# A hybrid decoder trunk on one core: VectorE and ScalarE of the last matrix product put in program order, its loads begun earlier, and the residual added in PSUM

## The chip, the cores and the metric

The kernel runs on one core of a Trainium2 chip. The metric is the device time of one execution in microseconds (us). A time worked on by the profiler ("the profiled execution") is given with its span, which reaches from the first to the last instruction.

The core has five engines with an instruction queue each: TensorE (PE in the rows, with its weight loads as PEld) multiplies into PSUM, VectorE (DVE) and ScalarE (ACT) do elementwise work, GpSimd (POOL) little here, and SyncE (SP) issues all DMA transfers.

## What is computed

One decoder layer in float32 on 1024 positions of width 1024: a token mixer, cross-attention, a gated MLP with a causal convolution, and a final RMSNorm. The change lies in the last two lines of this excerpt.

```python
def conv_ffn(xn, w_up, conv_w, conv_b, w_down):
    h = xn @ w_up                                   # 1024 x 5632
    hp = jnp.pad(h, ((0, 0), (CONV_WIDTH - 1, 0), (0, 0)))
    hc = conv_b + sum(conv_w[k] * hp[:, k:k + S] for k in range(CONV_WIDTH))
    gate, val = jnp.split(hc, 2, axis=-1)
    return (jax.nn.silu(gate) * val) @ w_down       # 2816 -> 1024
...
    h = h + conv_ffn(xn, ...)
return rmsnorm(h, final_norm_g)
```

## The kernel before

**Split operands.** A float32 product is done in three TensorE products: each operand is split into a high part (`hi`, a ScalarE copy that rounds, L150) and a low part (`lo = src - hi`, a VectorE subtraction, L151), and `mm3` (L138) adds hi·hi, hi·lo and lo·hi in PSUM. So before TensorE can take an operand, ScalarE and then VectorE have to pass over it. The first of three matmuls needs only `hi`, the second `lo`.

**The up phase** makes the MLP's inner activations in 11 chunks `c` of 256 features, for `kind` 0 (gate) and 1 (value). Each is seven products of one weight block by one block of activations (`pair`, L734; the names B11, B21, T2, T3, T1, T4, B22 are operand blocks that lie in `slot` buffers). After the seven products the convolution follows (`conv`: a ScalarE shift L700, two VectorE taps L701 and L702, then for kind 1 the gate product L707 and the store of the chunk to DRAM, L708).

**The down phase** multiplies these activations by `w_down`. It is a seven-product scheme of 2x2 blocks too: the products p1, p7, p6, p4, p5, p2 and p3 each run over the 11 chunks. Counted on, that is 77 steps, and this text numbers them 0 to 76 (p1 is 0 to 10, p7 11 to 21, p6 22 to 32, p4 33 to 43, p5 44 to 54, p2 55 to 65, p3 66 to 76). A step is 12 matmuls (`multiply`, four PSUM banks of three). The four banks `bank` and the four banks `val` take turns, product by product.

Per chunk there is a large buffer `G[c]` (four pieces of 128x512) and a small one `U[c]` (two pieces), which reuse the buffers of the up phase's operands. They are filled by `load_first` (two pieces), `load_second` (three) and `load_third` (one), 256 KB a piece, 66 pieces in all. VectorE then forms the sums that a product needs in place, by line L903 (`sub`), L913 and L924; three of these functions (`p6`, `p5`) also issue the reload of a piece.

**Order.** TensorE and SP run in program order throughout. VectorE and ScalarE are ordered by a scheduler, which places instructions by their dependencies and by `tc.high_priority()`. `run` (L936) asks for the operands of the next two steps, sums included, at high priority:

```python
        for c in range(NC - whole):
            ahead(2)
            w = ops.pop(c)
            for i in range(4):
                multiply(banks[i], w, i, fresh and c == 0, c == NC - 1, not fresh)
```

The operands go into four sets in turn (two pairs of `wb`, two pairs of `tb`). SP's order at the start is: the first loads of chunks 0 to 3, then the two stores of the last activations, then the rest.

**End.** After each product, `add_res` (L387) adds the four banks to the residual `res` in SBUF. At the end the last three steps are done bank by bank; for each bank follow `add_res`, a square with row sum (ScalarE L985), a small VectorE operation (L986), a power on GpSimd (L987), two scalings (ScalarE L988 and VectorE L989) and two stores (L992).

Of the kernel before, what the change touches and what calls it, by code (L numbers as in the profile page):

```python
# [15 lines left out]
P = 128  # L16
D = 1024
# [12 lines left out]
def kernel(ctx: ExitStack, tc: tile.TileContext, a, out: bass.AP):  # L30
# [842 lines left out]
    nset = [0]  # L873

    def operands(*srcs):

        i = nset[0] % 4
        nset[0] += 1
        if i < 2:
            hi, lo = wb[2 * i], wb[2 * i + 1]  # L880
        else:
            renew_temp(2 * i - 4, F32R)
            renew_temp(2 * i - 3, F32R)
            hi, lo = tb[2 * i - 4], tb[2 * i - 3]
        with tc.high_priority():
            if len(srcs) == 1:
                v = lambda x: x.rearrange("p (q n) -> p q n", q=2)
                split(srcs[0], v(hi), v(lo))
            else:
                for q in range(2):  # L890
                    split(srcs[q], hi[:, q * 512 : (q + 1) * 512], lo[:, q * 512 : (q + 1) * 512])
        return hi, lo
# [6 lines left out]
    def evict(t, n, banks, i):  # L899
        with tc.high_priority():  # L900
            add_res(4 * t + i, n, banks[i])

    sub = lambda o, x, y: nc.vector.tensor_tensor(o, x, y, ALU.subtract)  # L903

    def p1(c):
        return (G[c][:, 0:2],)

    def p7(c):
        sub(U[c], U[c], G[c][:, 0::3])
        return (U[c],)  # L910

    def p6(c):
# [3 lines left out]
        return (U[c],)  # L916

    def p4(c):
        sub(G[c][:, 1], G[c][:, 1], U[c][:, 1])
        return G[c][:, 2], G[c][:, 1]  # L920

    def p5(c):
# [4 lines left out]
        return (G[c][:, 0:2],)  # L927

    def p2(c):
        return G[c][:, 2], U[c][:, 1]  # L930

    def p3(c):
        sub(G[c][:, 2], G[c][:, 2], U[c][:, 0])
        return (G[c][:, 2:4],)

    def run(prep, banks, fresh, outs, steps=(), whole=0):  # L936

        ops = {}
        todo = list(range(NC))

        def ahead(n):
            while todo and len(ops) < n:
                c = todo.pop(0)
                with tc.high_priority():
                    ops[c] = operands(*prep(c))

        for c in range(NC - whole):
            ahead(2)
            w = ops.pop(c)
            for i in range(4):  # L950
                multiply(banks[i], w, i, fresh and c == 0, c == NC - 1, not fresh)
            for f in steps:
                f(c)
        ahead(whole)
        for i in range(4):
            for c in range(NC - whole, NC):
                multiply(banks[i], ops[c], i, False, c == NC - 1, not fresh)
            for t, n in outs:
                evict(t, n, banks, i)
            if whole:  # L960
                last(i)
# [3 lines left out]
    early = {}  # L965

    def free(c):
        return slot[big_tags[c]][:, :1024]

    def first_half(i):  # L970

        c = slice(0, 512)
        o, ss = free(4 + i), tiny()
        early[i] = free(8 + i // 2)[:, i % 2 * 512 : i % 2 * 512 + 512]
        nc.scalar.activation(o[:, c], res[i][:, c], AF.Square, accum_out=ss)
        sums[i] = tiny()
        nc.vector.tensor_scalar(sums[i], ss, D * EPS, None, ALU.add)
        tt(early[i], res[i][:, c], gF[:, c], ALU.mult)

    def last(i):  # L980
        o, r = free(4 + i), res[i]
        v, ss, rs = tiny(), tiny(), tiny()
        with tc.high_priority():
            c = slice(512, D)
            nc.scalar.activation(o[:, c], r[:, c], AF.Square, accum_out=ss)  # L985
            nc.vector.tensor_scalar(v, ss, sums[i], 1.0 / D, ALU.add, ALU.mult)  # L986
            nc.gpsimd.tensor_tensor(rs, v, mhalf, ALU.pow)  # L987
            nc.scalar.activation(o[:, :512], early[i], AF.Copy, scale=rs)  # L988
            nc.vector.scalar_tensor_tensor(o[:, c], r[:, c], rs, gF[:, c], ALU.mult, ALU.mult)  # L989
        for q in range(2):  # L990
            c = slice(q * 512, (q + 1) * 512)
            nc.sync.dma_start(out[i * P : (i + 1) * P, c], o[:, c])  # L992

    def whole_tile(i):
        o, r = free(i - 4), res[i]
        v, ss, rs = tiny(), tiny(), tiny()
        nc.scalar.activation(o, r, AF.Square, accum_out=ss)
        nc.vector.tensor_scalar(v, ss, 1.0 / D, EPS, ALU.mult, ALU.add)
        nc.gpsimd.tensor_tensor(rs, v, mhalf, ALU.pow)
        nc.vector.scalar_tensor_tensor(o, r, rs, gF, ALU.mult, ALU.mult)  # L1000
        nc.sync.dma_start(out[i * P : (i + 1) * P], o)

    def second_ahead(c):
        if c + 5 < NC:
            load_first(c + 5)
        load_second(c)

    def early_loads(q):
        if 1 <= q <= 4:
            load_first(q - 1)  # L1010

    for c in range(1, NC):
        pair(0, c)
        pair(1, c, early_loads if c == NC - 1 else None)
    load_first(4)
    run(p1, bank, True, [(0, 0)], [second_ahead])
    run(p7, val, True, [(1, 1)], [load_third])
# [66 lines left out]
```

## Time and profile before

| | |
|---|---|
| median of 3 runs | 1202.66 us (1202.23 to 1204.57) |
| profiled execution: its time | 1205.13 us |
| its span | 1203.4 us |
| TensorE busy | 1168.1 us (97%) |
| VectorE busy | 789.4 us (66%) |
| ScalarE busy | 512.1 us (43%) |
| DMA | 105.37 MB, 88 GB/s on average |
| mean granted TensorE clock | 0.988 of full |
| chain that ended last | TensorE 90%, DMA 4%, VectorE 4% |

Busy TensorE is not TensorE at its peak: the matmuls are pipelined and overlap, so the rows below are read by when matmuls start and by the idle time ahead of them. The down phase is the last fifth of the span; everything ahead of it has TensorE busy at 9 tenths or more of each slice.

### The profile page before, as it was taken

The numbers are of one execution on the slowest core, as the hardware profiler recorded it, in microseconds if no ns is written. First come the engines' busy times: TensorE is split into PE (matmuls) and PEld (weight loads), VectorE is DVE, ScalarE is ACT, GpSimd is POOL, SyncE is SP. The second block draws the span as 40 slices with busy tenths as digits, with TensorE's granted clock in tenths as the row PEclk, the third lists the DMA queues.
The fourth block names the chain that finished last, engine by engine and source line by source line (L and its number), as shares of the span: only waits on it lengthen the run. The fifth ranks groups of instructions, "written<-read, shape, count | busy, mean of one in ns | idle before, by whom it ended". The sixth has DMA issues, their size and how long they took to land.

```text
span 1203.4 us, 14229 instructions
## 1 busy us (share of the span) xinstructions
PE 1168.1 (97%) x5512; PEld 978.4 (81%) x5512; DVE 789.4 (66%) x1074; ACT 512.1 (43%) x811; POOL 34.2 (3%) x75
## 2 busy tenths in 40 slices
PE   9999999999999999999999999999999976799997
PEld 7888888899888888888888888888888865688885
DVE  5555852258534524459878878787887769866684
ACT  7422322246423412356545545455454532244543
POOL 1200100100000000000000000000000000000000
PEclk9999999999999999999999999999999988899999
DMA  9211131155100111101222132212322295124011
GB/s 350 91 44 52 53 106 68 39 174 175 37 1 1 55 68 36 36 1 35 88 88 79 62 105 88 88 61 79 105 88 88 88 357 202 62 76 135 1 70 70
DMA packets 43844, 105.37 MB, mean 88 GB/s; under 512 B 4992, under 2 KB 5120, under 8 KB 43776
## 3 DMA queue, kind: packets, MB, share of 16 engines
q1 hardware_dynamic: 43776, 104.46, 25.0%
q8 instruction: 43, 0.70, 0.2%
q14 instruction: 25, 0.20, 0.0%
HBM read 88.72 MB, written 15.73 MB: 87 GB/s over the span
## 4 chain that ended last, share of the span: by engine, by line
PE 90%; DMA 4%; DVE 4%; issue 1%; ACT 1%; SPq 0%; POOL 0%; POOLq 0%; ACTq 0%; DVEq 0%
PE sm L136 46%; PE bank L136 24%; PE big L136 18%; PE sm L144 2%; DMA slot<-in_w_down_dram 1%; DMA h<-act 1%; DMA slot<-act 1%; DVE wb L151 1%; DMA h<-in_w_down_dram 1%; DVE tb L151 0%; DVE h L913 0%; SPq L157 0%; DVE slot L924 0%; DMA h<-in_w_v_dram 0%; DVE slot L903 0%
## 5 line engine op out<-in xcount | busy, mean ns | idle before, releaser
L136 PE MATMUL sm<-slot,wb 128*128 128x512 f32 (+1 forms) x1176 | 219.6, 346 | 0.0
L150 ACT CAST wb<-raw 128x512 fp32r<-128x512 f32 (+1 forms) x178 | 113.5, 641 | 238.8 <-PE sm L136 59.5
L136 PEld LDWEIGHTS sm<-slot,wb 128*128 128x128 f32 x1176 | 188.6, 189 | 27.2
L136 PE MATMUL big<-slot,wb 128*128 128x512 f32 (+1 forms) x704 | 180.0, 377 | 0.0
L151 DVE TENSOR_TENSOR wb<-raw,wb 128x512 fp32r<-128x512 f32 (+1 forms) x178 | 126.3, 712 | 66.5 <-ACT wb L150 66.2
L136 PE MATMUL bank<-slot,wb 128*128 128x512 f32 x696 | 161.6, 389 | 0.0
L136 PEld LDWEIGHTS bank<-slot,wb 128*128 128x128 f32 x696 | 130.5, 188 | 27.0
L136 PEld LDWEIGHTS big<-slot,wb 128*128 128x128 f32 x704 | 125.5, 188 | 23.9 <-DVE tb L336 0.7
L136 PE MATMUL sm<-slot,slot 128*128 128x512 f32 x376 | 91.8, 395 | 1.2 <-ACT slot L150 1.2
L387 DVE TENSOR_TENSOR res<-res,sm 128x512 f32<-128x512 f32 x44 | 29.6, 687 | 95.9 <-PE sm L136 95.9
L136 PEld LDWEIGHTS sm<-slot,slot 128*128 128x128 f32 x376 | 71.5, 191 | 16.8 <-ACT slot L150 1.5
L136 PE MATMUL sm<-h,slot 128*128 128x512 f32 x264 | 66.0, 391 | 0.0
L701 DVE SCALAR_TENSOR_TENSOR slot<-tb,par,slot 128x1023 f32<-128x1023 f32 x44 | 56.3, 1282 | 10.7 <-ACT slot L700 9.7
L136 PE MATMUL big<-h,wb 128*128 128x512 f32 x160 | 62.3, 389 | 0.0
L136 PE MATMUL bank<-wb,wb 128*128 128x512 f32 x176 | 57.5, 409 | 2.8 <-DVE wb L151 2.8
L136 PEld LDWEIGHTS sm<-h,slot 128*128 128x128 f32 x264 | 49.3, 188 | 10.1
L136 PE MATMUL sm<-wb,wb 128*128 128x512 f32 x136 | 43.1, 398 | 14.7 <-DVE wb L151 14.7
L136 PE MATMUL bank<-tb,tb 128*128 128x512 f32 x176 | 54.6, 391 | 2.4 <-DVE tb L151 2.4
L702 DVE SCALAR_TENSOR_TENSOR slot<-tb,par,slot 128x1022 f32<-128x1022 f32 x44 | 56.2, 1278 | 0.0
L700 ACT ACTIVATE slot<-tb,par 128x1024 f32<-128x1024 f32 x44 | 54.7, 1244 | 3.3 <-DVE tb L737 2.6
L136 PE MATMUL bank<-h,wb 128*128 128x512 f32 x240 | 56.0, 389 | 0.0
L136 PE MATMUL sm<-h,wb 128*128 128x512 f32 x240 | 56.0, 389 | 0.0
(180 smaller groups left out, 1721.8 us busy)
## 6 DMA issues: line engine op xcount, KB each, us to landing
raw<-in_w_up_dram SPq DMA_DIRECT2D x88, 256.0 KB, 3.3
act<-h SPq DMA_DIRECT2D x22, 512.0 KB, 3.0
slot<-act SPq DMA_DIRECT2D x33, 256.0 KB, 5.4
slot<-in_w_down_dram SPq DMA_DIRECT2D x33, 256.0 KB, 5.4
h<-in_w_down_dram SPq DMA_DIRECT2D x20, 256.0 KB, 4.9
res<-in_x_dram SPq DMA_DIRECT2D x8, 512.0 KB, 10.2
raw<-in_w_pu_dram SPq DMA_DIRECT2D x8, 512.0 KB, 3.9
raw<-in_w_out_dram SPq DMA_DIRECT2D x8, 512.0 KB, 3.5
```

The costliest lines, as they stand in the source:

```text
L136: i = nc.tensor.matmul(o, l, r, start=start, stop=stop, skip_group_check=more)
L144: i = nc.tensor.transpose(o, i_, ident)
L150: copied[0] = nc.scalar.copy(hi, src)
L151: nc.vector.tensor_tensor(lo, src, f32(hi), ALU.subtract)
L387: nc.vector.tensor_tensor(r, r, ps, ALU.add)
L700: nc.scalar.activation(o, h, AF.Identity, bias=w(3), scale=w(2))
L701: stt(o[:, 1:], h[:, : S - 1], w(1), o[:, 1:], ALU.mult, ALU.add)
L702: stt(o[:, 2:], h[:, : S - 2], w(0), o[:, 2:], ALU.mult, ALU.add)
```

## The change

For the down phase and the last chunk of the up phase, VectorE and ScalarE are taken from the scheduler and run in program order as well. That order is then written out: in step `t`, the split of step `t + 3`, the sums for step `t + 5`, the matmuls of step `t`, and whatever a table `later` lists for `t` (evictions, loads, the parts of the final norm). The operand sets are given by a list `sets`, of which the first steps use three and then four. The last value chunk is written out too, with the down phase's first loads and splits between its products. Ahead of the last product, `seed` adds the residual to the accumulating PSUM banks; the last square and the last scaling read PSUM, and there is no last `add_res`.

```diff
+    sets = [(tb, 0), (wb, 0), (wb, 2)] * 2 + [(tb, 2)]
+    sets += [(tb, 0), (wb, 0), (wb, 2), (tb, 2)] * 18
...
-    def p7(c):
+    def sum7(c):
         sub(U[c], U[c], G[c][:, 0::3])
...
+    STEPS = 7 * NC
+    AHEAD, SUMS = 3, 5
...
+    def step(t):
+        k, c = divmod(t, NC)
+        banks, fresh = products[k][2:4]
+        w = ops.pop(t)
         for i in range(4):
+            multiply(banks[i], w, i, fresh and c == 0, c == NC - 1, not fresh)
+        for f, args in later[t]:
+            f(*args)
...
+    def seed(i):
+        tt(bank[i], bank[i], res[i][:, 512:], ALU.add)
...
+    def last_square(i):
+        v, ss, rs = tail[i] = tiny(), tiny(), tiny()
+        nc.scalar.activation(free(4 + i)[:, 512:], bank[i], AF.Square, accum_out=ss)
+        nc.vector.tensor_scalar(v, ss, sums[i], 1.0 / D, ALU.add, ALU.mult)
         nc.gpsimd.tensor_tensor(rs, v, mhalf, ALU.pow)
+    def last_scale(i):
+        nc.scalar.activation(o[:, :512], early[i], AF.Copy, scale=rs)
+        nc.vector.scalar_tensor_tensor(o[:, c], bank[i], rs, gF[:, c], ALU.mult, ALU.mult)
...
+    at(2, load_first, 10)
+    at(2, load_second, 10)
+    for c in range(3, 10):
+        at(c - 3, load_second, c)
+    for c in range(NC):
+        at(c + 8, load_third, c)
...
+    ctx.enter_context(tc.manual_schedule(engines={ET.DVE, ET.Activation}))
...
+    go(0, X, "B11")
+    load_first(0)
+    load_first(1)
+    nc.scalar.copy(c11, X)
...
+    for t in range(STEPS - 3):
+        reuse = sets[t + AHEAD] == sets[t]
+        if t == 1:
+            taps0()
+        if reuse:
+            step(t)
+        prepare_step(t + AHEAD)
+        if t == 1:
+            gate0()
+        sum_step(t + SUMS)
+        if not reuse:
+            step(t)
+    for i in range(4):
+        for t in range(STEPS - 3, STEPS):
+            multiply(bank[i], ops[t], i, False, t == STEPS - 1, True)
+        last_square(i)
+        if i:
+            last_scale(i - 1)
+    last_scale(3)
```

On SP, where the down phase's loads begin. Before: the first loads of chunk 3 (`slot_6558`), the two stores of the last activations, and then the first loads of chunks 4 and 5 and the second loads of chunk 0 (`h_0_6621`).

```order
L157 DMA slot_6558<-act_0_3737 128x512
L157 DMA slot_6558<-in_w_down_dram 128x512
L708 DMA act_1_3752<-h_1_4118 128x1024
L708 DMA act_0_3751<-h_0_4117 128x1024
L157 DMA slot_6599<-act_0_3739 128x512
L157 DMA slot_6599<-in_w_down_dram 128x512
L157 DMA slot_6618<-act_0_3741 128x512
L157 DMA slot_6618<-in_w_down_dram 128x512
L157 DMA h_0_6621<-act_0_3731 128x512
```

Now, the same engine around the same two stores: the first loads of chunk 9 (`slot_6626`) and the second loads of chunks 3 and 4 (`h_1_6647`, `slot_6517`, `h_0_6667`, `slot_6535`) stand ahead of the second store, and behind it the first loads of chunk 10 (`slot_6687`).

```order
L157 DMA slot_6626<-act_0_3749 128x512
L157 DMA slot_6626<-in_w_down_dram 128x512
L1065 DMA act_1_3752<-h_1_4118 128x1024
L157 DMA h_1_6647<-act_0_3737 128x512
L157 DMA h_1_6647<-in_w_down_dram 128x512
L157 DMA slot_6517<-in_w_down_dram 128x512
L157 DMA h_0_6667<-act_0_3739 128x512
L157 DMA h_0_6667<-in_w_down_dram 128x512
L157 DMA slot_6535<-in_w_down_dram 128x512
L1065 DMA act_0_3751<-h_0_4117 128x1024
L157 DMA slot_6687<-act_0_3751 128x512
L157 DMA slot_6687<-in_w_down_dram 128x512
```

The first loads of chunks 4 to 9 and the second loads of chunks 0 to 2 moved from behind both stores to ahead of them.

On VectorE, in the second half of p7 (steps 11 to 21). Before: the stretch that ends with the splits of step 18 (`tb_6939<-h_1_6770`, chunk 7) and step 17 (`wb_76<-h_0_6752`, chunk 6). L913 is a sum of p6, L924 one of p5 (steps 44 to 54), L903 the subtraction of any of these products; the split of step 20 (chunk 9, `h_1_6808`) stands three rows ahead of this piece.

```order
L913 TENSOR_TENSOR h_1_6808<-slot_6706,h_1_6808 128x512
L903 TENSOR_TENSOR slot_6558<-slot_6558,h_1_6688 128x512
L903 TENSOR_TENSOR h_1_6732<-slot_6618,h_1_6732 128x512
L903 TENSOR_TENSOR h_1_6808<-slot_6706,h_1_6808 128x512
L924 TENSOR_TENSOR slot_6506<-slot_6506,h_0_6621 128x512
L924 TENSOR_TENSOR slot_6706<-slot_6706,h_1_6808 128x512
L924 TENSOR_TENSOR slot_6599<-slot_6599,h_0_6709 128x512
L151 TENSOR_TENSOR tb_6939<-h_1_6770,tb_6938 128x1024
L924 TENSOR_TENSOR slot_6542<-slot_6542,h_0_6667 128x512
L913 TENSOR_TENSOR h_1_6770<-slot_6664,h_1_6770 128x512
L924 TENSOR_TENSOR slot_6685<-slot_6685,h_0_6788 128x512
L151 TENSOR_TENSOR wb_76<-h_0_6752,wb_75 128x1024
```

Now, on the same engine, the splits of steps 17 to 20: by the new buffers `h_0_6716` is chunk 6, `h_1_6734` chunk 7, `h_0_6752` chunk 8 and `h_1_6771` chunk 9. L899 is the subtraction of any sum, here p7's, and L387 an eviction of p1.

```order
L151 TENSOR_TENSOR wb_76<-h_0_6716,wb_75 128x1024
L899 TENSOR_TENSOR h_0_6752<-h_0_6752,slot_6623 128x1024
L387 TENSOR_TENSOR res_66<-res_66,bank_3730 128x512
L151 TENSOR_TENSOR tb_6701<-h_1_6734,tb_6700 128x1024
L899 TENSOR_TENSOR h_1_6771<-h_1_6771,slot_6626 128x1024
L151 TENSOR_TENSOR tb_6570<-h_0_6752,tb_6569 128x1024
L899 TENSOR_TENSOR misc<-misc,slot_6687 128x1024
L151 TENSOR_TENSOR wb_74<-h_1_6771,wb_73 128x1024
```

The splits now stand in the order of the steps, with one step's sums between two of them.

## Rows read from the trace of the kernel before

**Rows 1.** Busy time by stretch: PE, PEld, DVE, ACT, POOL, clock, DMA share, GB/s.
```profile
954.70:1194.60 239.90, 217.47 (x925) 177.04 (x924) 177.07 (x227) 90.95 (x121) 3.44 (x6) 0.95 0.33 118
954.70:1048.00 93.30, 70.87 (x280) 55.98 (x280) 78.41 (x93) 26.97 (x26) 0.00 (x0) 0.87 0.57 206
1048.00:1194.60 146.60, 146.59 (x647) 121.06 (x645) 98.67 (x135) 63.98 (x95) 3.44 (x6) 1.00 0.18 62
```

**Rows 2.** Timeline of PE, first to last matmul of the down phase: start, duration, [idle before].
```profile
954.75 0.39 PE L136 MATMUL bank<-wb 128*128 128x512 f32 x1
...
964.05 0.73 PE L136 MATMUL bank<-tb,tb 128*128 128x512 f32 x2 [0.75 <-DVE tb L151]
...
969.33 0.80 PE L136 MATMUL bank<-wb 128*128 128x512 f32 x1 [2.49 <-ACT wb L150]
970.59 1.22 PE L136 MATMUL bank<-wb,wb 128*128 128x512 f32 x2 [0.46 <-DVE wb L151]
...
973.32 1.06 PE L136 MATMUL bank<-wb,wb 128*128 128x512 f32 x2
...
989.40 0.90 PE L136 MATMUL bank<-wb,wb 128*128 128x512 f32 x2 [2.33 <-DVE wb L151]
...
1027.78 1.22 PE L136 MATMUL sm<-wb,wb 128*128 128x512 f32 x2 [14.74 <-DVE wb L151]
...
1047.62 0.73 PE L136 MATMUL bank<-tb,tb 128*128 128x512 f32 x2 [1.64 <-DVE tb L151]
...
1193.98 0.61 PE L136 MATMUL bank<-wb,wb 128*128 128x512 f32 x2
```

**Rows 3.** Timeline of ACT: the splits of step 27 and of step 76.
```profile
1050.52 1.05 ACT L150 CAST tb<-h 128x1024 fp32r<-128x1024 f32 x1 [3.68 <-PE bank L136]
...
1183.75 1.05 ACT L150 CAST wb<-slot 128x1024 fp32r<-128x1024 f32 x1 [1.67 <-PE bank L136]
```

**Rows 4.** Timelines of ACT and DVE around step 17.
```profile
1004.74 1.05 ACT L150 CAST wb<-h 128x1024 fp32r<-128x1024 f32 x1 [1.71 <-PE sm L136]
1008.65 3.70 DVE L913 TENSOR_TENSOR h<-slot,h 128x512 f32<-128x512 f32 x6
1026.49 1.24 DVE L151 TENSOR_TENSOR wb<-h,wb 128x1024 fp32r<-128x1024 f32 x1
```

**Rows 5.** Waits of SP's queue (total us, times, longest), then timeline of ACT.
```profile
SPq L708 <- DVE h L707: 19.0, 2, 17.0
968.24 1.04 ACT L150 CAST wb<-slot 128x1024 fp32r<-128x1024 f32 x1 [5.50 <-DMA slot<-in_w_down_dram]
```

**Rows 6.** Timeline of DVE in the last up chunk, around its convolution's start.
```profile
952.23 0.69 DVE L737 TENSOR_TENSOR tb<-tb,sm 128x512 f32<-128x512 f32 x1 [0.34 <-PE sm L136]
...
954.46 1.28 DVE L701 SCALAR_TENSOR_TENSOR slot<-tb,par,slot 128x1023 f32<-128x1023 f32 x1 [1.54 <-ACT slot L700]
```

**Rows 7.** DMA issues (KB each, us to landing), then timeline of SP's queue.
```profile
act<-h SPq DMA_DIRECT2D x22, 512.0 KB, 3.0
slot<-act SPq DMA_DIRECT2D x33, 256.0 KB, 5.4
995.35 7.10 SPq L157 DMA_DIRECT2D slot<-act  x11
```

**Rows 8.** Timeline of DVE: two splits one right behind the other.
```profile
1045.21 1.23 DVE L151 TENSOR_TENSOR wb<-h,wb 128x1024 fp32r<-128x1024 f32 x1
1046.34 1.23 DVE L151 TENSOR_TENSOR tb<-h,tb 128x1024 fp32r<-128x1024 f32 x1
```

**Rows 9.** Timeline of DVE and ACT at the end: the last bank.
```profile
1196.13 0.75 DVE L989 SCALAR_TENSOR_TENSOR slot<-res,small,raw 128x512 f32<-128x512 f32 x1 [0.66 <-POOL small L987]
1196.80 0.68 DVE L387 TENSOR_TENSOR res<-res,bank 128x512 f32<-128x512 f32 x1
1197.51 0.63 ACT L985 ACTIVATE slot<-res 128x512 f32<-128x512 f32 x1 [0.66 <-DVE res L387]
1199.14 0.75 DVE L989 SCALAR_TENSOR_TENSOR slot<-res,small,raw 128x512 f32<-128x512 f32 x1 [0.66 <-POOL small L987]
```

More of the change, by code (lines that the diff above doesn't have):

```diff
@@ L977, in first_half @@
         nc.vector.tensor_scalar(sums[i], ss, D * EPS, None, ALU.add)
[L978 to L998, printed above, removed]
-        nc.gpsimd.tensor_tensor(rs, v, mhalf, ALU.pow)
[L1000 to L1006, printed above, removed]
@@ new lines @@
+    at(2, load_first, 10)
[4 more added lines that the diff above has]
+        at(c + 8, load_third, c)
+    at(20, load, gF, a["gF"].broadcast_to([P, D]))
+    for k in range(6):
+        for i in range(4):
+            for t, n in products[k][4]:
+                at((k + 1) * NC + i, add_res, 4 * t + i, n, products[k][2][i])
+    for i in range(4):
+        at(57 + 2 * i, square, 4 + i)
+        at(58 + 2 * i, power, 4 + i)
+        at(59 + 2 * i, scaled, 4 + i)
+        at(59 + i, seed, i)
+        at(67 + i, first_half, i)
@@ L1027, with go, add, conv_parts @@
-    run(p3, bank, False, [(0, 1)], whole=3)
+        if c < NC - 1:
+            pair(1, c)
+    ctx.enter_context(tc.manual_schedule(engines={ET.DVE, ET.Activation}))
+    c10 = NC - 1
+    X, Z, Y, V = val
+    (c11, c12), (c21, c22) = (hl(H[1][j]) for j in range(2))
+    def go(q, o, xname, start=True):
+        product(o, ready.pop((1, c10, q)), xname, start, True, not start)
+        prepare()
+    def add(o, x):
+        tt(o, o, x, ALU.add)
+    def conv_parts(j):
+        h, f = H[1][j], NF + 2 * c10 + j
+        w = lambda q: pconv[:, f, q : q + 1]
+        o = half(0, j)
+        stt = nc.vector.scalar_tensor_tensor
+        sg = half(7, j)
+        def shift():
+            nc.scalar.activation(o, h, AF.Identity, bias=w(3), scale=w(2))
+        def taps():
+            stt(o[:, 1:], h[:, : S - 1], w(1), o[:, 1:], ALU.mult, ALU.add)
+            stt(o[:, 2:], h[:, : S - 2], w(0), o[:, 2:], ALU.mult, ALU.add)
+        def gate():
+            tt(sg, sg, o, ALU.mult)
+            nc.sync.dma_start(act[c10][j], sg)
+        return shift, taps, gate
@@ new lines @@
+    shift0, taps0, gate0 = conv_parts(0)
+    shift1, taps1, gate1 = conv_parts(1)
+    go(0, X, "B11")
+    load_first(0)
+    load_first(1)
+    nc.scalar.copy(c11, X)
+    go(1, Z, "B21")
+    load_first(2)
+    load_first(3)
+    add(c11, Z)
+    go(2, X, "T2", False)
+    load_first(4)
+    load_first(5)
+    nc.scalar.copy(c21, X)
+    go(3, Y, "T3")
+    for c in range(3):
+        load_second(c)
+    add(c21, Y)
+    prepare_step(0)
+    go(4, X, "T1", False)
+    nc.scalar.copy(c22, X)
```

145 lines of the change are left out of this document (75 added, 70 removed).

## The prediction

> **What bounds the kernel now.** I read the busy time by stretch first. From the first matmul of the down phase to its last, 239.9 us pass, and they fall into two parts [rows 1]: up to 1048 us TensorE is busy for 70.87 of 93.3 us at a mean granted clock of 0.87; behind it for 146.59 of 146.6 us at 1.00. So whatever a change of order can give back lies in the first 93 us. VectorE is busy for 177.1 us of the whole stretch, less than TensorE needs, so it isn't the bound by its sum; by its order it may be.
>
> The pace without stalls comes from ScalarE. In the second part its split of each step is released by TensorE's end of a step, so the distance of two splits is the length of a step: from step 27 to step 76 there are 49 steps in 1183.75 - 1050.52 = 133.23 us, 2.72 us each [rows 3]. The phase has 77 steps: 77 x 2.72 = 209.44 us, plus 0.16 us by which the last matmul (0.39 us) outlasts the distance to a next one (2.72/12 = 0.23). It took from 954.75 to 1193.98 + 0.61 = 1194.59, 239.84 us [rows 2]. The excess is 239.84 - 209.60 = 30.24 us.
>
> Then TensorE's timeline, for where the excess lies. There are six idle pieces, and the rows of the group are all of them: 0.75 + 2.49 + 0.46 + 2.33 + 14.74 + 1.64 = 22.41 us [rows 2]. [...] Each idle microsecond so cost 7.83/22.41 = 0.35 us more, and I price idle time at 1.35.
>
> What ended the long gap is the `lo` of step 17. ScalarE had its `hi` done at 1004.74 + 1.05 = 1005.8; VectorE made the `lo` at 1026.49, and in between it did work for later products, such as six sums of p6 (step 22 on) in one row [rows 4]. It was never waiting in that time; the order held the split back. The three gaps at 964 to 971 have another origin: SP waited 17.0 us at the first store of the last activations, with the first loads of chunks 4 to 10 behind it in its queue, and ScalarE then waited 5.50 us for step 4's data [rows 5].
>
> **The change, part by part.**
>
> *Order of VectorE and ScalarE.* It removes no work but the last four `add_res`; each split and sum remains. Costs for VectorE, from two splits in a row: 1.23 us each, 1.13 from start to start [rows 8]; 128x512 sums start 0.60 apart (six in 3.70, each 0.70) [rows 4]. Per step this makes 1.13 + 1.13 = 2.26 us in p7's range, 1.13 + 1.20 = 2.33 where p6's sums are made, and 0.60 more in the four steps that carry an eviction, 2.93 at most. Over 2.72 by 0.21, four times, VectorE falls behind by 0.8 us and makes it up at 0.39 a step. The densest place is steps 59 to 63 (p2's split 1.20, a seed 0.60, a scaling 1.2 every other step, from step 61 a sum 0.60): about 14.05 us against 5 x 2.72 = 13.6, 0.45 behind. How much lateness can it bear? With four operand sets, ScalarE's split of step t+3 starts as step t starts on TensorE, `hi` takes 1.05 [rows 3] and `lo` 1.23, so it is ready 2.28 us into step t; the second matmul of t+3 wants it at 3 x 2.72 + 0.23 = 8.39. Slack 6.1 us, against 0.8 needed. So the 14.74, 2.33 and 1.64 us gaps go, and nothing is late next: sums stand five steps ahead, two before their split.
>
> *The start.* With three sets the slack is smaller, so I follow VectorE with full durations. The add of the T4 product starts at 952.23 and the taps at 954.46, as before [rows 6]: taps to 954.46 + 2 x 1.28 = 957.0, `lo` of step 2 to 958.25, gate product to 959.5, `lo` of 3 to 960.7, the other chunk half's taps to 963.3, `lo` of 4 to 964.5, gate to 965.7, `lo` of 5 to 967.0, of 6 to 968.2. They are wanted at 954.75 + 2.72 t + 0.23: 960.4, 963.1, 965.9, 968.6, 971.3. Slacks 2.2, 2.4, 1.4, 1.6 and 3.1. ScalarE isn't later: for step 4 it starts at the end of step 1, 960.2, and ends at 961.2. Steps 0 and 1 are split within the last chunk, before TensorE comes to them. So 0.75 us of the gaps go too.
>
> *Loads.* Firsts up to chunk 9 and seconds up to chunk 2 no longer stand behind the stores; their buffers are free as each product of the last chunk ends. SP's loads cost 0.68 us from issue to issue when the engines are full (eleven in 7.10) and land 5.4 us after issue [rows 7]. The first buffers are free as the first of the last chunk's seven products ends, 954.75 - 6 x 2.72 = 938.4. The 29 pieces from then on (12 firsts, 9 seconds, 8 firsts) would be issued by 958.1 and landed by 963.5 if nothing but the DMA engines held them; the firsts of chunk 4 are among the first twelve and wait for the third product's end at 943.9, so step 4's data are there before 955. That removes 2.49 and 0.46 us. Behind the second gate (965.7) the store takes 3.0, and chunk 10's first pieces 0.68 + 5.4: landed at 974.9, split at 977.2, wanted at 954.75 + 27.2 + 0.23 = 982.2, slack 5.0. Seconds of 5 to 9 end 20 issues after 968.8, at 982.4, landed 987.8; the sum of step 20 is due in step 15, at 995.6. All covered; all 66 pieces take 44.9 us of the 59.8 that p1 and p7 last.
>
> *Seeds and tail.* Four adds into PSUM during p2 cost nothing: VectorE's slack above hides them, and `val`, not `bank`, is in use. Before, the last bank's add came 1196.80 - 1194.59 = 2.2 us after TensorE's end, because VectorE stood at the third bank's scaling, which waited for GpSimd; the square started at 1197.51, the scaling at 1199.14, the end came at 1203.4 [rows 9]. Now the square can start at TensorE's end + 0.04 (the gap seen between add and square), the scaling 1.63 us later, the end 4.26 us after: 5.93 instead of 8.81 us, 2.88 gained. No row shows a scaling from PSUM; the nearest, an add with a PSUM source, takes 0.68 us against 0.70 for sums from SBUF [rows 4, 9], so from nothing to 0.1 us more. Four stores now queue close together instead of two; the bound is two issues, 2 x 0.68 = 1.4 us, and below it nothing. I take nothing: the third bank's stores go out while the last scaling runs. [...]
>
> Sum: 1203.4 - 30.24 - 2.88 = 1170.3 us of span. The profiled execution's time was 1.7 us above its span and 2.47 above the median of the runs; so 1202.66 - 33.1 = **1169.5 us**.
>
> **Rivals.**
>
> *A. Bubbles at the start remain.* The chain from 952 to 968 us has 1.4 us of slack at its tightest, and hand-overs between engines that I left out stand in it. If two to four idle microseconds are left, 2.7 to 5.4 us: 1172 to 1175. Against it: durations were taken in full, though starts are closer.
>
> *B. The early gaps were the loads' and stay.* The same bytes move, and the store that chunk 10 reads back is still in the queue. If 0.75 + 2.49 + 0.46 + 2.33 = 6.03 us remain: 8.1 us, 1177.6. Against it: the slacks of 5 us and more.
>
> *C. The long gap comes back.* If sums still crowd out splits once, 14.74 x 1.35 = 19.9 us: 1189. Against it: a split is never behind more than one step's sums.
>
> *D. Slower: one wait holds everything behind it.* Free of the scheduler, the engines can't go round a late load. SP's queue has the second gate's store ahead of chunk 10's and most seconds; VectorE's sum of p7 then waits with all later splits behind it. Each microsecond past the 5.0 of slack costs 1.35. The gain of 33.1 is gone at 24.5 idle, that is, if the gate product ends at 965.7 + 5.0 + 24.5 = 995 instead of 965.7. For it: SP did wait 17.0 us at such a store [rows 5]. Against it: the pieces that are due first no longer stand behind these stores. Time past that point: over 1205.
>
> [...]
>
> **How the numbers follow.** My forecast 0.70, A 0.15, B 0.06, C 0.05, D 0.03, no change 0.01. Within 0.2% (2.4 us) a measurement of this kernel tells nothing from no change. The forecast's own range is 1167 to 1172: 2.4 us for measurement, or the bounds of the tail. The forecast and A together leave 0.15 out, so the range goes to A's top with measurement, 1177. Faster 0.96 (forecast, A, B, C), same 0.01, slower 0.03.
>
> **What would show it.** Right: TensorE without an idle piece from about 955 to 1164 us, clock 1.00 throughout, ScalarE's splits 2.72 us apart, and 6 us from the last matmul to the end. Wrong: an idle piece released by VectorE's L151 before 970 (A), by ScalarE behind a DMA wait before 990 (B), or by a split behind a sum that waits for a load (D). The forecast fails too if the up phase, which I take as unchanged, gets longer.

## The result and the profile after

The changed kernel takes 1172.64 us (median of 4 runs, 1170.84 to 1172.9) against 1202.45 us before (median of 4, 1201.67 to 1204.57). The ratio is 0.9746, with a 95% interval of 0.9729 to 0.9763: it is faster, by 29.8 us. The profiled execution of after took 1170.84 us and has a span of 1169.1 us.

The page of after, its head and the chain that ended last (shares of the span by engine, followed back from the last instruction):

```profile
span 1169.1 us, 14245 instructions
...
PE 97%; DVE 1%; DMA 1%; ACT 0%; issue 0%; SPq 0%; DVEq 0%; ACTq 0%
```

The windows of after over the down phase, cut in the same way as [rows 1], with the same columns:

```profile
952.90:1162.60 209.70, 209.68 (x926) 173.28 (x924) 176.16 (x229) 92.82 (x123) 3.84 (x7) 1.00 0.34 121
952.90:1046.20 93.30, 93.30 (x414) 77.24 (x413) 83.36 (x94) 39.53 (x43) 0.00 (x0) 1.00 0.51 183
1046.20:1162.60 116.40, 116.38 (x514) 96.03 (x512) 92.80 (x136) 53.28 (x81) 3.84 (x7) 1.00 0.20 71
```

TensorE is busy for all of the first 93.3 us, where it was busy for 70.87, and the granted clock is 1.00 there instead of 0.87. VectorE's busy time is the same but for 0.9 us. So the same work stands in 30 us less.

The timeline of PE in after, first and last matmul of the down phase:

```profile
952.98 0.39 PE L136 MATMUL bank<-tb 128*128 128x512 f32 x1
...
1161.96 0.61 PE L136 MATMUL bank<-wb,wb 128*128 128x512 f32 x2
```

No row between the two carries an idle time, that is, TensorE waited for nothing that the profile shows. The phase lasts from 952.98 to 1162.57, 209.59 us; before, the rows of [rows 2] stood in it.

The timeline of VectorE in after: the `lo` of step 2 and the second gate product (L1064), and the stretch around step 17 (L151 is the `lo` of a split, L899 a subtraction of a sum, L387 an eviction):

```profile
955.03 1.22 DVE L151 TENSOR_TENSOR wb<-slot,wb 128x1024 fp32r<-128x1024 f32 x1
...
962.09 1.22 DVE L1064 TENSOR_TENSOR h<-h,slot 128x1024 f32<-128x1024 f32 x1
...
992.84 1.22 DVE L151 TENSOR_TENSOR wb<-h,wb 128x1024 fp32r<-128x1024 f32 x1
993.98 1.22 DVE L899 TENSOR_TENSOR h<-h,slot 128x1024 f32<-128x1024 f32 x1
995.11 0.68 DVE L387 TENSOR_TENSOR res<-res,bank 128x512 f32<-128x512 f32 x1
995.71 1.22 DVE L151 TENSOR_TENSOR tb<-h,tb 128x1024 fp32r<-128x1024 f32 x1
```

The timeline of ScalarE in after: the splits of step 10, step 17 and step 18:

```profile
972.22 1.06 ACT L150 CAST tb<-slot 128x1024 fp32r<-128x1024 f32 x1 [1.67 <-PE bank L136]
...
991.30 1.06 ACT L150 CAST wb<-h 128x1024 fp32r<-128x1024 f32 x1 [1.66 <-PE sm L136]
994.02 1.05 ACT L150 CAST tb<-h 128x1024 fp32r<-128x1024 f32 x1 [1.66 <-PE sm L136]
```

Step 17's `hi` ends at 992.36 and its `lo` starts at 992.84; before, 20.7 us lay between the two [rows 4]. ScalarE waits for TensorE to free a set, 2.72 us from split to split, and no longer for data: even chunk 10, step 10, the last to be loaded, is there before its set is free.

The end of after on ScalarE, VectorE, GpSimd and SP's queue (L999 is the square from PSUM, L1000 the small operation of VectorE, L1001 the power, L1006 and L1007 the scalings, L1010 the stores):

```profile
1161.59 0.55 POOL L1001 TENSOR_TENSOR small<-small,mhalf 128x1 f32<-128x1 f32 x1 [1.49 <-DVE small L1000]
...
1162.20 3.84 SPq L1010 DMA_DIRECT2D out_dram<-slot  x6
1162.61 0.60 ACT L999 ACTIVATE slot<-bank 128x512 f32<-128x512 f32 x1 [0.74 <-PE bank L136]
...
1163.34 0.21 DVE L1000 TENSOR_SCALAR small<-small 128x1 f32<-128x1 f32 x1 [1.17 <-ACT slot L999]
1163.46 1.50 DVE L1007 SCALAR_TENSOR_TENSOR slot<-bank,small,raw 128x512 f32<-128x512 f32 x2
1163.63 0.55 POOL L1001 TENSOR_TENSOR small<-small,mhalf 128x1 f32<-128x1 f32 x1 [1.49 <-DVE small L1000]
1164.21 0.72 ACT L1006 ACTIVATE slot<-slot,small 128x512 f32<-128x512 f32 x1 [0.30 <-POOL small L1001]
```

From the last matmul's end to the span's end 6.56 us pass, instead of 8.82 [rows 2, 9].

From profile to profile the span is 1203.4 - 1169.1 = 34.3 us shorter. This comes from three places: the down phase 239.84 - 209.59 = 30.25, the end 2.26, and the start of the down phase, 954.75 - 952.98 = 1.77, which lies ahead of everything that was changed.

### The profile page after: what moved, and what is told of

Its sections match the earlier page's. It is cut to its first block, busy times and chain, and to the rows that moved or that the text cites. A ratio compares the mean times of both kernels' runs of the same rounds, so it can differ in the third digit from the quotient of the medians.

```text
span 1169.1 us, 14245 instructions
## 1 busy us (share of the span) xinstructions
PE 1158.3 (99%) x5512; PEld 973.3 (83%) x5512; DVE 787.2 (67%) x1074; ACT 511.7 (44%) x811; POOL 34.1 (3%) x75
## 4 chain that ended last, share of the span: by engine, by line
PE 97%; DVE 1%; DMA 1%; ACT 0%; issue 0%; SPq 0%; DVEq 0%; ACTq 0%
PE sm L136 49%; PE bank L136 28%; PE big L136 18%; PE sm L144 2%; DVE slot L151 0%; DMA raw<-in_w_out_dram 0%; DMA h<-in_w_v_dram 0%; ACT slot L150 0%; DVE h L151 0%; DVE h L154 0%; DVE wb L151 0%; DVE slot L1007 0%; ACT tb L542 0%; DVE h L342 0%; ACT wb L150 0%
## 5 line engine op out<-in xcount | busy, mean ns | idle before, releaser
L151 DVE TENSOR_TENSOR wb<-raw,wb 128x512 fp32r<-128x512 f32 (+1 forms) x178 | 126.0, 711 | 65.3 <-ACT wb L150 65.2
L387 DVE TENSOR_TENSOR res<-res,sm 128x512 f32<-128x512 f32 x44 | 30.2, 686 | 93.6 <-PE sm L136 93.6
L701 DVE SCALAR_TENSOR_TENSOR slot<-tb,par,slot 128x1023 f32<-128x1023 f32 x42 | 53.7, 1281 | 9.2 <-ACT slot L700 8.2
L136 PE MATMUL bank<-wb,wb 128*128 128x512 f32 x176 | 54.2, 389 | 0.0
L700 ACT ACTIVATE slot<-tb,par 128x1024 f32<-128x1024 f32 x42 | 52.2, 1245 | 3.2 <-DVE tb L737 2.6
L702 DVE SCALAR_TENSOR_TENSOR slot<-tb,par,slot 128x1022 f32<-128x1022 f32 x42 | 53.6, 1277 | 0.0
L136 PEld LDWEIGHTS bank<-h,wb 128*128 128x128 f32 x240 | 45.0, 188 | 9.4
```

What stands on the lines that cost most here:

```text
L136: i = nc.tensor.matmul(o, l, r, start=start, stop=stop, skip_group_check=more)
L151: nc.vector.tensor_tensor(lo, src, f32(hi), ALU.subtract)
L387: nc.vector.tensor_tensor(r, r, ps, ALU.add)
L700: nc.scalar.activation(o, h, AF.Identity, bias=w(3), scale=w(2))
L701: stt(o[:, 1:], h[:, : S - 1], w(1), o[:, 1:], ALU.mult, ALU.add)
L702: stt(o[:, 2:], h[:, : S - 2], w(0), o[:, 2:], ALU.mult, ALU.add)
```

## The experiments

The theory is the prediction's: the order of VectorE and ScalarE gave back the large gap, the loads the small ones, PSUM the end. Its rivals are that one of these parts does all of it, and that the slacks that the prediction worked out are wrong. In the table, "first matmul" is when the down phase starts, "excess" is the time from first to last matmul less 209.60 us, "idle" the sum of TensorE's idle pieces in it, "end" the time from the last matmul's end to the span's end.

| kernel | time, us | first matmul | idle | excess | end |
|---|---|---|---|---|---|
| before | 1202.45 (median) | 954.75 | 22.41 | 30.24 | 8.82 |
| after | 1172.64 (median) | 952.98 | 0 | 0 | 6.56 |
| order, late loads | 1178.86 (median) | 954.73 | 3.64 | 5.94 | 6.56 |
| scheduler, early loads | 1201.63 (median) | 952.72 | 20.68 | 27.54 | 8.82 |
| old end | 1172.42 | 953.36 | 0 | 0 | 7.76 |
| eight steps' sums at once | 1180.63 | 956.99 | 3.84 | 5.77 | 6.57 |
| late gate | 1174.18 | 955.16 | 0.77 | 1.15 | 6.56 |
| two operand sets | 1176.31 | 953.28 | 1.77 | 5.12 | 6.57 |
| stores from two queues | 1171.1 | 953.48 | 0 | 0 | 6.31 |
| before, once more | 1199.84 | 953.4 | 21.08 | 26.3 | 8.82 |
| sums four steps ahead | 1190.45 | 953.08 | 12.02 | 19.5 | 6.56 |
| last scaling from PSUM | 1173.81 | 954.75 | 0 | 0 | 7.76 |

Times without "median" are of one run; the other columns are of one profile each. Since the down phase starts up to 4 us earlier or later with nothing changed ahead of it, single runs are compared by their excess and their end, not by their time. The spans for the last column are taken to a hundredth.

### The new order with the old loads

The loads go back to their old places: the first loads of chunks 0 to 3 one chunk per product, the rest behind the first store, five pieces a step. They are not quite as late as before: the second store now stands behind the loads of two steps, where all of these stood behind both stores.

```diff
+        if c + 5 < NC:
+            at(c, load_first, c + 5)
+        at(c, load_second, c)
+        at(c + 11, load_third, c)
...
     gate1()
+    load_first(4)
```

> The changed kernel, with VectorE and ScalarE in program order, but the loads in the order of the kernel before: the first loads of chunks 0 to 3 one chunk per product of the last up chunk, chunk 4's behind the first gate store, and then in each step of p1 the first pieces of chunk c + 5 together with the second pieces of chunk c. That is five pieces a step, 5 x 0.68 = 3.4 us against 2.72 us for a step. Theory (the early loads carry the gaps at 964 to 990): first pieces come later by 0.7 us each step, TensorE is idle 4 to 6 us in p1, in pieces released by ScalarE behind a DMA wait, 1178 to 1181 us. Rival 1 (order alone gives all): no idle piece, 1172.6. Rival 2 (all six early microseconds come back with the loads): 6.0 idle, 1181.

It took 1178.86 us (1177.59 to 1180.2, 4 runs), a ratio to before of 0.9806 (0.9784 to 0.9828). ScalarE's timeline, with its waits for data, in this kernel:

```profile
970.30 1.05 ACT L150 CAST tb<-slot 128x1024 fp32r<-128x1024 f32 x1 [3.61 <-DMA slot<-in_w_down_dram]
...
974.85 1.05 ACT L150 CAST tb<-slot 128x1024 fp32r<-128x1024 f32 x1 [3.51 <-DMA slot<-in_w_down_dram]
```

And PE's timeline there:

```profile
977.21 0.74 PE L136 MATMUL bank<-tb,tb 128*128 128x512 f32 x2 [0.76 <-DVE tb L151]
...
981.18 0.74 PE L136 MATMUL bank<-wb,wb 128*128 128x512 f32 x2 [0.76 <-DVE wb L151]
```

Late data reach TensorE as a late `lo`: the releaser named is VectorE, and the DMA stands one engine further back. Seven pieces, none over 0.76 us and one of them released by ScalarE, are all that is left of the 22.41; 4 to 6 us were expected, and 3.64 came. So the order and the new end give 1202.45 - 1178.86 = 23.6 us together, 2.26 of it at the end, and the early loads the other 6.2. Chunk 4's first load is issued at 959.60 us here and at 963.31 in before, with the same start of the down phase; so a part of the 23.6 may be the loads' still.

### The new loads with the old order

Against the kernel before, `run` and the scheduler stay; only the loads' places become those of the change (but the first loads of chunks 8 and 9 stand behind the first store).

```diff
+        for c in {0: (0, 1), 1: (2, 3), 2: (4, 5), 5: (6, 7), 6: (8, 9)}.get(q, ()):
+            load_first(c)
+        if q == 3:
+            for c in range(3):
+                load_second(c)
```

> The kernel before, with its scheduler for VectorE and ScalarE and its old end, but the loads as early as in the changed kernel. Theory (the order is the main thing; the schedule puts the split of step 3 behind that of step 6, and that of step 13 behind those of steps 14 to 16 and nine sums): idle pieces of about 5 us at step 3 and 7 us at step 13, 10 to 16 us in all, with the slow clock 13 to 22 us over the changed kernel, and 2.3 us for the end: 1188 to 1197 us. Rival 1 (the loads were the cause): all idle pieces up to 990 gone and the long one gone with them, 1175. Rival 2 (loads matter only for the early gaps): the 14.7 us piece and 1.6 stay, 1197.

It took 1201.63 us (1200.39 to 1204.48, 10 runs), a ratio of 0.9996 (0.9983 to 1.0008): no difference. The expectation of a gain was wrong. PE's timeline:

```profile
966.67 0.79 PE L136 MATMUL bank<-tb 128*128 128x512 f32 x1 [4.87 <-ACT tb L150]
...
1005.40 1.22 PE L136 MATMUL sm<-wb,wb 128*128 128x512 f32 x2 [8.54 <-DVE wb L151]
...
1037.98 1.22 PE L136 MATMUL bank<-tb,tb 128*128 128x512 f32 x2 [6.32 <-DVE tb L151]
```

No split of ScalarE waits for a load in this kernel's down phase, so the loads were early enough. But the scheduler made another order from the same work, and other gaps with it: before step 13's split, which ended the 8.54 us, VectorE did the splits of steps 14 to 16 and sums between them. That it put them there because their data came earlier is likely, but not shown. So early loads are worth 6.2 us on top of the order and nothing without it.

### Eight steps' sums at once

The sums of steps 22 to 29, sixteen operations, are done in step 16 ahead of step 19's split: a copy of what made the old long gap.

```diff
+        if t == 16:
+            for u in range(22, 30):
+                sum_step(u)
         prepare_step(t + AHEAD)
...
+        if not 22 <= t + SUMS < 30:
+            sum_step(t + SUMS)
```

> The changed kernel, but the sums of steps 22 to 29 (16 operations, 8 x 1.20 = 9.6 us) are all made in step 16, ahead of the split of step 19, instead of one step's sums in each of eight steps. Theory (a split bears 6.1 us of lateness): VectorE comes to the burst 0.7 us into step 16, the split ends 0.7 + 9.6 + 1.2 = 11.5 us into it, it is wanted at 8.39, so one idle piece of 3.1 us ahead of step 19's second matmul, released by VectorE's split, and 1 us more of slow matmuls. Rival 1 (no slack: splits wait and TensorE waits with them): about 9.6 us idle. Rival 2 (slack larger than worked out): none.

PE's timeline in this kernel, behind the burst:

```profile
1012.90 0.73 PE L136 MATMUL sm<-tb,tb 128*128 128x512 f32 x2 [3.84 <-DVE tb L151]
...
1013.80 1.05 PE L136 MATMUL sm<-tb,tb 128*128 128x512 f32 x2
```

And its window there:

```profile
1008.00:1018.00 10.00, 6.16 (x20) 4.61 (x19) 9.48 (x12) 2.62 (x3) 0.00 (x0) 0.83 0.76 244
```

One idle piece of 3.84 us came. It understates the delay by 0.16, since the last matmul ahead of it outlasts the distance to a next one: 4.0 late. The slack of 6.1 us was about right. In the 10 us around the piece the mean clock was 0.83 of full, and 5.77 - 4.0 = 1.77 us of excess are slow matmuls (two take 1.05 us, against 0.61 to 0.62 ahead of the piece and behind the slow ones) and the restart, where 1 us was expected: 1.5 us of excess for each idle one, near the prediction's price of 1.35 (by chance, as the section on the prediction shows).

### Sums four steps ahead instead of five

```diff
-    AHEAD, SUMS = 3, 5
+    AHEAD, SUMS = 3, 4
```

> The changed kernel with the sums four steps ahead instead of five, splits still three ahead. In VectorE's queue the sum of a step then stands right ahead of its own split, and ScalarE's part lies between the two, so VectorE waits for it: sum 1.20, ScalarE 1.05, split 1.23, 3.48 us a step against 2.72, and 0.60 more with an eviction. Theory (the five of the change is what keeps the two engines from taking turns): idle pieces small and many in p7, p6 and p5, released by VectorE and ScalarE, 15 to 25 us in all, 1190 to 1200 us. Rival 1 (three steps of slack hide it): none, 1172. Rival 2 (the 6.1 us of slack hide it in p7, and p4 gives it back): under 8 us.

It took 1190.45 us, as expected, with 21 idle pieces of 12.02 us in all, where 15 to 25 us were expected. VectorE's timeline, p6's range (L906 and L899 are the sums):

```profile
1020.36 1.22 DVE L151 TENSOR_TENSOR tb<-h,tb 128x1024 fp32r<-128x1024 f32 x1 [1.19 <-ACT tb L150]
1021.50 0.68 DVE L906 TENSOR_TENSOR h<-slot,h 128x512 f32<-128x512 f32 x1
1022.10 0.68 DVE L899 TENSOR_TENSOR h<-slot,h 128x512 f32<-128x512 f32 x1
1023.98 1.23 DVE L151 TENSOR_TENSOR wb<-h,wb 128x1024 fp32r<-128x1024 f32 x1 [1.20 <-ACT wb L150]
```

And PE's:

```profile
1018.02 0.74 PE L136 MATMUL bank<-tb,tb 128*128 128x512 f32 x2 [0.56 <-DVE tb L151]
...
1021.64 0.74 PE L136 MATMUL bank<-tb,tb 128*128 128x512 f32 x2 [0.56 <-DVE tb L151]
```

A step's sum now stands right ahead of its own split, and the work goes to and fro between the two engines: VectorE sums, ScalarE takes 1.05 and two hand-overs, VectorE subtracts. 1.14 + 1.28 + 1.20 = 3.62 us from split to split instead of 2.72, with VectorE idle for a third of it. The fifth step ahead, which the prediction took only for a reserve ("two before their split"), is what lets VectorE work while ScalarE does.

### The second gate product, and all that hangs on it, late

Rival D in small: the gate product whose store chunk 10 reads back goes from step 1 to step 6, and chunk 10's and five chunks' second loads with it.

```diff
+    at(6, load_first, 10)
+    at(6, load_second, 10)
     for c in range(3, 10):
+        at(c - 3 if c < 5 else 6, load_second, c)
...
+        if t == 6:
             gate0()
```

> The changed kernel, but the last gate product and its store are made in step 6 instead of step 1, and the loads of chunk 10 and the second pieces of chunks 5 to 9 stand behind that store in SP's queue. This is rival D of the prediction made to happen, some 10 us late where it bears 5. By rows of the changed kernel the gate would end at 973.0, the store land at 976, chunk 10's first pieces at 980 to 982, its split end at 982.3 to 984.3; wanted at 980.4. Theory: one idle piece of 2 to 4 us ahead of step 10, released by ScalarE behind a DMA wait, with 1 us of slow matmuls, and none where the sums of chunks 5 to 9 stand (their pieces come 2.04 us a chunk, a step takes 2.72). Rival 1 (the first-in-first-out queue spreads it: sums of p7 hold back further splits): more idle pieces in steps 11 to 15, over 8 us in all. Rival 2: none, the slack is larger.

The store and the first load behind it on SP, and ScalarE's split of step 10, in this kernel:

```profile
975.16 0.33 SPq L1065 DMA_DIRECT2D act<-h  x1
...
977.85 0.33 SPq L157 DMA_DIRECT2D slot<-act  x1
...
981.22 1.05 ACT L150 CAST tb<-slot 128x1024 fp32r<-128x1024 f32 x1 [8.48 <-DMA slot<-in_w_down_dram]
```

Counted from the first matmul, the product came 9.6 us later than in after, and cost one idle piece of 0.77 us at step 10 and 1.15 us of excess; 2 to 4 us idle were expected. By the prediction's slack of 5.0 it would have cost (9.6 - 5.0) x 1.35 = 6.2. From the product's end (975.13) to the end of the split it took 981.22 + 1.05 + 1.23 - 975.13 = 8.4 us where the prediction had 977.2 - 965.7 = 11.5: with an empty queue the data were there 3.0 us after the issue of the second piece, not 5.4 as in a full one [rows 7]. So what rival D describes does happen, but from a point further off than the prediction put it.

### Two operand sets instead of four

```diff
+    sets = [(tb, 0), (wb, 0)] * 38 + [(wb, 2)]
+    AHEAD, SUMS = 2, 5
```

> The changed kernel with two operand sets in turn instead of four, and splits two steps ahead instead of three. A set is free only when step t ends, so the split of step t + 2 is ready 2.72 + 2.28 = 5.0 us after step t's start, wanted at 5.67: slack 0.7 instead of 6.1. Theory: no idle piece in most steps, but in those where an eviction, a seed or a scaling of the final norm (0.6 to 1.9 us) stands ahead of the split: 4 to 8 us in all, most of it in steps 59 to 69. Rival 1 (four sets aren't needed): none. Rival 2 (hand-overs between engines use the 0.7 us too): some idle in each step, over 15 us.

It took 1176.31 us, excess 5.12. Two of the rows of PE with idle time:

```profile
962.22 0.73 PE L136 MATMUL bank<-wb,wb 128*128 128x512 f32 x2 [0.39 <-DVE wb L151]
...
1160.00 0.74 PE L136 MATMUL bank<-wb,wb 128*128 128x512 f32 x2 [0.76 <-DVE wb L151]
```

Of 1.77 visible idle us, 1.38 lie in the last three steps, which are done bank by bank and so want the last step's operands three steps early; the dense steps 59 to 69, where most of it was expected, show no idle piece. The rest of the excess is spread over delays too short to leave an idle piece. So the larger slack is worth some 5 us of excess, in one run, and most of the gain doesn't need it.

### The end: without the residual in PSUM

No `seed`; the last `add_res`, the square and the scaling read `res` in SBUF, in the new order.

```diff
+        add_res(i, 1, bank[i])
+        nc.scalar.activation(free(4 + i)[:, 512:], res[i][:, 512:], AF.Square, accum_out=ss)
...
+        nc.vector.scalar_tensor_tensor(o[:, c], res[i][:, c], rs, gF[:, c], ALU.mult, ALU.mult)
...
-        at(59 + i, seed, i)
```

> The changed kernel without the seeds: the last product's banks are added to the residual in SBUF again, ahead of each square, which reads SBUF, as does the last scaling; VectorE and ScalarE stay in program order. From the last matmul to the end it was 8.8 us before the change and 6.5 after. Theory (most of the 2.3 us came from VectorE's order, which kept the last add waiting 2.2 us, and the seed takes away only one add of 0.70): 7.2 us. Rival (the residual in PSUM gives it all): 8.8 us.

The end of this kernel (L387 is the last add, L1002 the power, L1008 the scalings):

```profile
1163.44 0.68 DVE L387 TENSOR_TENSOR res<-res,bank 128x512 f32<-128x512 f32 x1
...
1165.04 0.74 DVE L1008 SCALAR_TENSOR_TENSOR slot<-res,small,raw 128x512 f32<-128x512 f32 x1
1165.20 0.98 POOL L1002 TENSOR_TENSOR small<-small,mhalf 128x1 f32<-128x1 f32 x1 [1.27 <-DVE small L1001]
...
1166.22 0.75 DVE L1008 SCALAR_TENSOR_TENSOR slot<-res,small,raw 128x512 f32<-128x512 f32 x1 [0.44 <-POOL small L1002]
```

The end is 7.76 us: of the 2.26 gained, the order gives 1.06, since the last add starts 0.49 us after TensorE's last matmul instead of 2.2. The residual in PSUM gives 1.20; this shows in the end alone, since the one time of this kernel, 1172.42 us, is no longer than the median of after. The end is longer than the 7.2 us expected, and most of the reason is in the third row: GpSimd's power takes 0.98 us, beside a scaling of the bank before, where it took 0.55 in after. From the power's start to the scaling that waits for it, 1.02 us pass here and 0.58 in after.

### The end: last scaling from PSUM

The same kernel, but the last scaling reads the bank. The bank holds no residual here, so the kernel leaves the residual out of the last output columns.

```diff
-        nc.vector.scalar_tensor_tensor(o[:, c], res[i][:, c], rs, gF[:, c], ALU.mult, ALU.mult)
+        nc.vector.scalar_tensor_tensor(o[:, c], bank[i], rs, gF[:, c], ALU.mult, ALU.mult)
```

> As the run with the old tail (adds and squares in SBUF), but the last scaling on VectorE reads the PSUM bank, so the residual is left out of the last output columns. There the power on GpSimd took 0.98 to 0.99 us while VectorE's scaling from SBUF ran beside it, against 0.55 before and after the change. Theory (an operation of VectorE with two SBUF sources holds GpSimd up): 0.55 again, and the end 0.4 us shorter, 7.3 instead of 7.75. Rival (the longer power comes from something else in that kernel, such as the adds): 0.98 again, 7.75.

The scalings of the last two banks and the power in this kernel:

```profile
1166.42 1.50 DVE L1008 SCALAR_TENSOR_TENSOR slot<-bank,small,raw 128x512 f32<-128x512 f32 x2
1166.59 0.55 POOL L1002 TENSOR_TENSOR small<-small,mhalf 128x1 f32<-128x1 f32 x1 [1.71 <-DVE small L1001]
```

The power is back at 0.55 us: the first half of the theory holds. The end is not shorter (7.76 in both): the last scaling ends 0.44 us nearer to the last add's start, but the stores then take 4.18 us to the end instead of 3.75. The four last stores stand close together, and what is won ahead of them is lost in them; the next run shows why.

### The end: stores from two queues

```diff
+        for q, engine in ((1, nc.sync), (0, nc.scalar)):
             cq = slice(q * 512, (q + 1) * 512)
+            engine.dma_start(out[i * P : (i + 1) * P, cq], o[:, cq])
```

> The changed kernel, with one of the two stores of each of the last four banks issued from ScalarE's queue instead of SP's. From the last matmul to the end it was 6.5 us, against 5.9 forecast; from the last scaling's end to the end 4.1 us against 3.5 before the change. Theory (the stores queue up at SP's issue, four within 2 us): 5.9 to 6.1 us. Rival (the DMA engines or the landing set it): 6.5.

The end is 6.31 us instead of 6.56. With half of the stores on ScalarE's queue, 0.25 us are won, so SP's issuing is a small part of what the stores lost. The rest is the transfer. The windows over the packets of the last stores: the last two in before, the last four in after and in this kernel (the last two columns are the DMA engines' busy share and GB/s):

```profile
1200.72:1202.24 1.52, 0.00 (x0) 0.00 (x0) 0.00 (x0) 0.00 (x0) 0.00 (x0) 0.50 0.92 345
```

```profile
1165.06:1167.96 2.90, 0.00 (x0) 0.00 (x0) 0.00 (x0) 0.00 (x0) 0.00 (x0) 0.52 0.97 362
```

```profile
1165.29:1168.21 2.92, 0.00 (x0) 0.00 (x0) 0.18 (x1) 0.27 (x1) 0.00 (x0) 0.58 0.96 359
```

In before the stores of the third bank were done when the last two began. In after all four go one behind the other, and the DMA engines are full for 2.90 us; two queues don't change that. In all three kernels the span ends 1.18 us behind the last packet. So the end hangs on when the third bank's stores begin. In the two kernels of the sections before, the packets take 2.90 us too, and they begin 3.68 us behind the last matmul in both.

### Before, once more

The kernel before, unchanged, for a second profile of it.

> The kernel before once more, unchanged, for a second profile. The first one's time was 2.5 us above the median of its runs. Theory (the idle pieces hang on when loads land, and differ from run to run): first to last matmul of the down phase 236 to 240 us, with the long idle piece of 14 to 15 us unchanged, since only the order sets it, and the differences in the pieces up to 990. Rival: the down phase takes 239.8 us again and the difference lies ahead of it.

This execution took 1199.84 us. PE's timeline, the long gap:

```profile
1023.35 1.22 PE L136 MATMUL sm<-wb,wb 128*128 128x512 f32 x2 [13.44 <-DVE wb L151]
```

The gap is 13.44 us where it was 14.74 and was expected unchanged, there are eight idle pieces where there were six, and the excess is 26.3 us against 30.24. So the order alone doesn't set the long gap's length.

## Why the prediction was right

The time of 1172.64 us lies in the range (1167 to 1177) and 3.1 us above the 1169.5 that was forecast. It is 0.6 us above the forecast's own range (1167 to 1172) and falls where rival A was put (1172 to 1175), so that the range holds it is owed to A's top. But A's mark, an idle piece released by L151 before 970, isn't in the trace: the forecast's mechanism is what happened, and some of its sizes were off.

**The down phase** is right to 0.01 us: 209.59 instead of 209.60, with no idle piece and a clock of 1.00 in both stretches. The excess of 30.24 us went as a whole.

**VectorE's lateness.** The slack of 6.1 us was tested from outside, and 4.0 us of delay came out where 3.1 idle were expected. The chain at the start ran as followed, and a little ahead: with the start shifted by 1.77 us, `lo` of step 2 was forecast to end at 956.5 and ended at 956.25, the second gate product at 963.9 and 963.31.

**The loads.** All in time, and chunk 10 with more slack than worked out. Of the three gaps at 964 to 971 that the prediction puts down to the loads, the two of step 4 were theirs [rows 5]. The first, 0.75 us at step 3, was VectorE's: in before, step 3's `hi` waited 4.86 us for a tap of the last convolution (L702), which VectorE did at its place in the order:

```profile
961.67 1.06 ACT L150 CAST tb<-slot 128x1024 fp32r<-128x1024 f32 x1 [4.86 <-DVE slot L702]
```

The kernel with late loads has small gaps, at steps 4 and 6 to 10 (excess 5.94, where B put 8.1). What the prediction didn't see is that the loads alone are worth nothing.

**The end** was sized at 5.93 us and is 6.56. The square starts 0.04 us behind the last matmul, as forecast, and the scaling 1.60 later (forecast 1.63); the step that was off is "I take nothing" for four stores close together. From the scaling's start to the end 4.93 us pass instead of 4.26, within the bound of 1.4. The third bank's stores don't go out while the last scaling runs: the first packet of them moves at 1165.06, when that scaling has just ended, and the last bank's stores share the DMA engines with them. The third bank's scaling could start no earlier than 1163.46, since in VectorE's order it stands behind the last bank's small operation (1163.34), for which VectorE sat idle for 1.17 us, though the third bank's power was done at 1161.59 + 0.55 = 1162.14. The other order of these two was not tried. The scaling from PSUM takes 0.75 us, as from SBUF [rows 9]; so of the surplus of up to 0.1 us that the prediction allowed, nothing is seen.

**From span to median** is where most of the 3.1 us lies. The sum, 1170.3 us of span, is 1.2 above the profiled span of after: 1.77 by the earlier start, less the 0.6 of the end. But then the whole saving of 33.1 us, read from an execution 2.47 us above its median, was taken from the median. The excess isn't the same in each execution of before: 30.24 in one at 1205.13 us, 26.3 in one at 1199.84. Halfway between, where the median lies, it is an estimated 28.3, which with 2.26 at the end makes 30.6 us; 29.8 were measured. The phase without stalls doesn't vary (209.59 to 209.60 in the four profiles of kernels that have no stalls left). So the sum of span should have gone to the time by adding the 1.7 us that lie around the span: 1172.0.

**The price** of 1.35 per idle microsecond has its mechanism wrong, though the sum doesn't need it. The 7.83 us in it are 30.24 - 22.41, what the excess of before has beyond idle time. Slow matmuls have a part in it: two take 1.06 us at 973.32, with a granted clock of 0.50 from 972 to 974 us, and 0.61 at the end [rows 2], in the stretch with 1.00 [rows 1]. But these slow matmuls go with a piece, not with its length. Without stalls 11 matmuls take 11/12 x 2.72 = 2.49 us. In before, the first matmuls of the steps behind the pieces of 2.33 and of 14.74 us [rows 2], 11 matmuls on, are these:

```profile
993.61 0.39 PE L136 MATMUL bank<-tb 128*128 128x512 f32 x1
...
1031.77 0.39 PE L136 MATMUL sm<-tb 128*128 128x512 f32 x1
```

993.61 - 989.40 = 4.21 us behind the short piece and 1031.77 - 1027.78 = 3.99 behind the long one are 1.7 and 1.5 us more. So the long gap cost some 16.4 us, 1.1 for each idle one, and rival C's 19.9 was too much. Short pieces cost by another way. In the kernel with late loads seven pieces of 3.64 us in all cost 5.94, 1.6 for each idle one, with no slow matmul: each piece hides 0.16 us of overlap and takes about 0.12 more to start again (two matmuls 0.74 instead of 0.62), and 3.64 + 7 x 0.28 = 5.6. (Six pieces make some 1.7 of the 7.83 us.) By this reckoning, too, most of the 19.5 of the kernel with sums four steps ahead is there: 12.02 + 21 x 0.28 = 17.9.

## What to carry to other kernels

When an engine that others wait for is never idle in a gap, look at what it did in that time: here VectorE did work due later, and writing out the order, with the new end, gave 23.6 of the 29.8 us, while earlier data without the order gave nothing. Follow each chain over two engines through (sum, `hi`, `lo`): a step more of distance between two of its links was worth 18 us, more than the loads. Where several stores end a kernel, add up their transfer: here it kept the DMA engines busy at 0.97 to the end, and a last scaling that ended sooner gave nothing back. When a stalling kernel's saving is read from one profile, predict the new time from the new sum, not by subtracting from the median, since here the stalls differed from run to run and the work didn't.

## What was not expected of the hardware

**GpSimd beside VectorE.** A power of 128x1 took 0.98 to 0.99 us while VectorE scaled from two SBUF operands, and 0.55 when one of them lay in PSUM, in the same place of the same order. The first is the kernel without the residual in PSUM, the second the one with the last scaling from PSUM; the difference is 0.43 us, and what makes it was not shown.

**The clock behind short gaps.** Twenty-one idle pieces, most of some 0.57 us, and seven of up to 0.76, left the granted clock at 1.00 in the kernels with sums four steps ahead and with late loads; one of 3.84 us, in the kernel with eight steps' sums at once, was followed by slow matmuls, two of which take 1.05 us, against 0.62, with a granted clock of 0.83 over the 10 us around it.

**The start of the down phase** lies between 952.72 and 956.99 us in twelve profiles, with nothing changed ahead of the last up chunk. The windows of the first 30 us, of after (first line) and of the kernel with eight steps' sums at once:

```profile
0.00:30.00 30.00, 27.41 (x120) 22.91 (x121) 15.81 (x29) 22.36 (x35) 3.53 (x26) 1.00 0.94 356
```

```profile
0.00:30.00 30.00, 26.81 (x103) 21.96 (x104) 15.67 (x28) 20.14 (x32) 3.54 (x26) 1.00 0.92 346
```

TensorE got through 120 matmuls in one and 103 in the other while the DMA engines were busy at 0.9. Over the twelve, those with 117 to 120 start the down phase at 952.72 to 953.48, those with 110 to 112 at 954.73 to 955.16, that with 103 at 956.99. Two executions of the same kernel differ in it too: before had 111 and 954.75, and 117 and 953.4 once more. So some 4 us of the time are settled while the first loads run; what makes these differ was not tried.
